# A list scheduler's model of its engines: a port shared by VectorE and GpSimd, and estimates of other lengths

## The chip, the cores and the metric

One core of one Trainium2 chip runs the whole kernel as one launch. Its engines are TensorE (PE in the profile, with PEld for the weight loads beside it), VectorE (DVE), ScalarE (ACT), GpSimd (POOL) and SyncE (SP, which here issues DMAs). Each engine works through its own instructions strictly in the order in which the program holds them, and waits on semaphores for the others. The metric is the device time of one execution in microseconds (us), less is better.

## The reference

Two transformer blocks over one sequence of 256 positions and 1024 channels, in fp32.

```
h    = rms_norm(x) @ w_in            # first block: two convolution mixers (kernels of 3 and 31), gated
x   += w_mix_out(sigmoid(gate_sc) * y_sc + sigmoid(gate_cf) * y_cf)
x   += w_xo(cross_attention(q = rms_norm(x) @ w_q, k, v = rms_norm(mem) @ w_kv))
# PEER layer: 128 x 128 = 16384 experts, 8 heads, the best 16 of each head
s    = (rms_norm(x) @ w_pq) . subkeys ; top 16 of each half, then top 16 of the 256 sums
g    = softmax(best scores)
x   += sum over the chosen experts of gelu(h . u[e]) * g * v[e]
# second block: sliding-window attention with ALiBi and sinks, latent attention with rotary angles
x   += rmsnorm((sigmoid(g_a) * out_a @ w_o_a + sigmoid(g_b) * out_b @ w_o_b) @ w_out)
x   += rmsnorm(square(relu(rmsnorm(x) @ w_up)) @ w_down)
```

The kernel does not gather experts. It computes all 16384 products `h . u[e]` (128 units U of 128 experts each), multiplies them by a gate matrix that is zero for experts that were not chosen, and multiplies by all of v (128 units V).

## The kernel before, in words

**Units.** Weights come in units of 128x1024 fp32 (`w`, one DMA of 512 KB on SP's queue). fp32 products are made out of halves: ACT copies a unit to a rounded `wh` (L288), and GpSimd or VectorE subtracts it from `w` to get the rest, `wl` (L292). PE then does 24 matmuls of 128x256 for a unit: 16 with `wh` against the high and low half of the activations, 8 with `wl`. Three buffers each of `w`, `wh` and `wl` let the splits run up to three units ahead.

**Stages,** in the order in which PE meets them: the projections of the first block with the convolutions on VectorE (L607), the cross attention, the PEER queries, the top-16 search on VectorE, 128 U units (matmuls with `hA`, `hB`; ACT makes the gelu into `Ah`, L1234), 128 V units (matmuls with `zz`, which ACT and VectorE split from `Ah`, L241 and L238), then the second block: attention, its gates `se0`, the output products, and the MLP's 64 units.

**select(t)** (L1161 to L1203), for t = 0 and 1 (128 positions each): VectorE and an Exp on ACT turn the chosen 16 of each head into softmax gates, then four times compare (L1179), multiply (L1182) and reduce (L1185) 1024 columns; PE transposes the results (L1192), ACT and VectorE copy them to `selT`. Inside `choose()` select(1) follows select(0).

**Gates** (`gbatch`, L1251 to L1268): for 8 positions VectorE builds one-hot `ohJ` (L1251), `ohI` (L1253) and two products gI (L1256); PE does 16 matmuls of 128x64 (L1264); VectorE multiplies the result into `Ah` (L1268). There are 32 such batches for each half of the experts: half 0 is spawned behind U unit 63 and needs both selects, and V unit 0 needs half 0; half 1 is spawned behind U unit 127, and V unit 64 needs half 1. Two lanes of batches alternate.

**positions()** (L1319 to L1392): rotary angles and distances for the second block, on VectorE with two Sin on ACT, spawned at V unit 72. `x1_tile(n)`, the first step of the second block, comes behind a `need` for them and for the last `zz`.

**Who goes first.** The order of each engine's instructions is not written by hand. A list scheduler (`Sched`) in Python builds it when the program is made. Each chain of steps is a generator of `Op`s; an Op has an engine (or several to choose from) and an estimated cost. The scheduler keeps a virtual time for each engine, `vt`; the step with the lowest estimated start plus priority is emitted next. Splits have priority -200, gates 300, `choose()` 600, `positions()` 1500, convolutions 1500 and more (larger is later). The loop over units calls `sch.pe(...)`, which first emits everything whose estimated start lies before PE's virtual time, and then the unit's matmuls. `need` emits until an event exists. So the costs decide what stands ahead of what on every engine, and nothing on the chip reorders it.

Of the kernel before, what the change touches and what calls it, by code (L numbers as in the profile page):

```python
# [19 lines left out]
F32 = mybir.dt.float32  # L20
# [50 lines left out]
class Sched:  # L71
# [16 lines left out]
    def est(self, co):  # L88
        op = co.op
        t = co.ready if op.chain else co.last  # L90
        for d in op.deps:
            e = self.ev.get(d)
            if e is None:
                return None
            if e > t:
                t = e
        if op.eng == "pe":
            t += self.SLACK
        if isinstance(op.eng, str):
            return max(t, self.vt[op.eng]), op.eng, op.cost  # L100
        best = None
        for eng, cost, bias in op.eng:
            st = max(t, self.vt[eng])
            if best is None or st + cost + bias < best[0]:
                best = (st + cost + bias, st, eng, cost)
        return best[1:]

    def emit(self, co, st, eng, cost):
        op = co.op
        if isinstance(op.eng, str):  # L110
            op.fn()
        else:
            op.fn(eng)
        self.vt[eng] = st + cost
        fin = st + cost + self.LAT
        if op.chain:
            co.last = co.ready
        co.ready = max(co.ready, fin)
        if op.ev is not None:
            self.ev[op.ev] = fin  # L120
        co.op = next(co.gen, None)
        if co.op is None:
            self.cos.remove(co)

    def pick(self, horizon):
        best = None
        for co in self.cos:
            e = self.est(co)
# [61 lines left out]

def c_pool(n):
    return 150 + 2.1 * n


def c_mm(n, count=1):
    return count * (max(n, 64) / 2.4 + 2.5)
# [4 lines left out]
def tile_kernel(ctx, tc, A, out):  # L201
# [33 lines left out]


# [234 lines left out]
    def hl(H, L, src, n, hev, lev):  # L471

        yield Op("act", c_act(n), act(H, src, AF.Copy), ev=hev)
        yield Op("dve", c_dve(n), lambda: V.tensor_tensor(L, src, H.bitcast(F32), op=OP.subtract), ev=lev)  # L474

    def hl_gain(H, L, src, g, n, hev, lev, deps=()):
        yield Op("act", c_act(n, 1), act(H, src, AF.Copy, scale=g), deps=deps, ev=hev)
        yield Op("dve", c_dve(n, 1),
# [107 lines left out]
    def mulR(p, R, dst, rdep, ev=None):  # L586
        return Op("dve", c_dve(S), tt(dst, p[:, :S], R, OP.mult), deps=[rdep], ev=ev)
# [37 lines left out]
    def post_g(j):  # L625
        def g(p):
# [7 lines left out]
            yield Op("dve", c_dve(S, 1),  # L634
# [16 lines left out]
    def post_x(j):  # L651
        def g(p):
# [4 lines left out]
            yield Op("dve", c_dve(S), tt(b[:, 2:2 + S], p[:, :S], scc[j], OP.mult), deps=[("scc", j)])  # L657
# [115 lines left out]
    def post_k(n):  # L773
        def g(p):
            yield Op("act", c_act(S), act(kHL[:, 0, n], p[:, :S], AF.Copy))
            yield Op("dve", c_dve(S), tt(kHL[:, 1, n], p[:, :S], kHL[:, 0, n].bitcast(F32), OP.subtract),
# [35 lines left out]
    def post_v(n):  # L812
        def g(p):
# [4 lines left out]
            yield Op("dve", c_dve(512), tt(L, src, H.bitcast(F32), OP.subtract), ev=("v", n))  # L818
# [60 lines left out]
    for key, j in order:  # L879
# [6 lines left out]
        else:  # L886
            go(u)
# [16 lines left out]
    def post_sc(n):  # L904
        def g(p):
            d = gates["gs"][:, n]
            yield Op("dve", c_dve(S), tt(d, p[:, :S], d, OP.mult), deps=[("gs", n)], ev=("m1", n))
# [64 lines left out]
    def head_xa(h):  # L972
# [15 lines left out]
        yield Op("dve", c_dve(512), lambda: V.tensor_reduce(mx[:, 0:2], b["s"].rearrange("p (t m) -> p t m", t=2),  # L988
# [21 lines left out]
        yield Op("dve", c_dve(512), lambda: V.tensor_tensor(  # L1010
# [16 lines left out]
        yield Op("dve", c_dve(512), lambda: V.tensor_tensor(  # L1027
# [110 lines left out]
    def top16(val, idx, src, tmp, n, ev=None, deps=()):  # L1138
        yield Op("dve", c_dve(n), lambda: V.max(val[:, 0:8], src), deps=deps)
        yield Op("dve", c_dve(n), lambda: V.max_index(idx[:, 0:8], val[:, 0:8], src), chain=False)  # L1140
        yield Op("dve", c_dve(n), lambda: V.match_replace(tmp, val[:, 0:8], src, LOW), chain=False)
        yield Op("dve", c_dve(n), lambda: V.max(val[:, 8:16], tmp))  # L1142
        yield Op("dve", c_dve(n), lambda: V.max_index(idx[:, 8:16], val[:, 8:16], tmp), ev=ev)  # L1143
# [12 lines left out]
    def select(t):  # L1156
# [8 lines left out]
        yield Op("dve", c_dve(128), lambda: V.tensor_reduce(sm, g3, op=OP.add, axis=AX.X))  # L1165
# [9 lines left out]
        for q, (pos, dst) in enumerate(((AFi, IF), (BFi, JF))):  # L1175
            for c in range(2):
# [8 lines left out]
                yield Op("dve", c_dve(1024), lambda eq=eq, dst=dst, c=c: V.tensor_reduce(  # L1185
# [15 lines left out]
        yield Op("dve", c_dve(128), lambda: V.scalar_tensor_tensor(  # L1201
# [41 lines left out]
    def gbatch(hh, t0, pool):  # L1243
# [209 lines left out]
    def x1_tile(n):  # L1453
        yield Op("dve", c_dve(S), tt(x1[:, n], xr[:, n], vacc[n // 2][:, (n % 2) * S:(n % 2 + 1) * S], OP.add),
# [17 lines left out]
    def x1_stats():  # L1472
# [15 lines left out]
        for n in range(8):  # L1488
            yield Op("dve", c_dve(S, 1), lambda n=n: V.scalar_tensor_tensor(
# [78 lines left out]
    def post_kr(p):  # L1568
# [13 lines left out]
        for q in range(4):  # L1582
# [3 lines left out]
            yield Op("dve", c_dve(S), lambda r=r, q=q: V.tensor_tensor(  # L1586
# [9 lines left out]
    def post_ka(p):  # L1596
        t = p[:, :S]
        yield mulR(p, RR, t, "RR")
        for q in range(2):
# [3 lines left out]
            yield Op("dve", c_dve(S), lambda r=r, q=q: V.tensor_tensor(  # L1603
                kaM[r, 1, q], t[r], kaM[r, 0, q].bitcast(F32), op=OP.subtract), ev="ka" if q == 1 else None)

    def post_va(p):
# [12 lines left out]
        yield Op("dve", c_dve(S), lambda: V.tensor_tensor(  # L1619
# [23 lines left out]
    def tail(lane, pev, free, scale):  # L1643
# [4 lines left out]
        for i in range(2):  # L1648
            yield Op("dve", c_dve(256 - 128 * i), lambda i=i: V.tensor_reduce(
# [19 lines left out]
        yield Op("dve", c_dve(384), lambda: V.tensor_tensor(  # L1669
            pT[:, 1], b[:, 0:384], pT[:, 0].bitcast(F32), op=OP.subtract), ev=("pt",) + pev)  # L1670

    def head_a(h, lane, pev, free):
# [15 lines left out]
        yield Op("dve", c_dve(384), lambda: V.scalar_tensor_tensor(  # L1688
# [29 lines left out]
    def outs(pairs, group):  # L1718
        b = LB[2 * group]
        for kind, i in pairs:  # L1720
# [15 lines left out]
            for q in range(2):  # L1736
# [3 lines left out]
                yield Op("dve", c_dve(S), lambda r=r, q=q: V.tensor_tensor(  # L1740
# [42 lines left out]
    def post_gab(j, key):  # L1783
        def g(p):
            dst = sg[key]
            yield Op("dve", c_dve(S), lambda: V.tensor_tensor(dst[:, j], p[:, :S], RR, op=OP.mult), ev=(key, "raw", j))
# [25 lines left out]
    def post_kn(n, p):  # L1812
        for q in range(2):
# [3 lines left out]
            yield Op("dve", c_dve(S), lambda r=r, q=q: V.tensor_tensor(  # L1817
# [3 lines left out]
    def post_vb(s, p):  # L1821
        yield Op("act", c_act(512), lambda: ACT.activation(vbP[:, 0, s], p, AF.Copy))
        yield Op("dve", c_dve(512), lambda: V.tensor_tensor(vbP[:, 1, s], p, vbP[:, 0, s].bitcast(F32),
# [170 lines left out]
    def fin():  # L1994
# [4 lines left out]
        for n, c in ((0, 2), (2, 2), (4, 2), (6, 2)):  # L1999
            y, xx = yg[:, n:n + c], xn[:, n:n + c]  # L2000
            yield Op("dve", c_dve(c * S, 1), tt(y, y, r.to_broadcast([128, c, S]), OP.mult),
# [109 lines left out]
```

## Time and profile before

| | us |
|---|---|
| median of 3 runs (lowest, highest) | 1803.94 (1802.5, 1808.71) |
| the profiled execution | 1811.32 |
| its span in the trace | 1809.5, granted clock 0.954 |
| PE busy | 1688.5 (93% of the span) |
| DVE, ACT, POOL busy | 1222.8 (68%), 803.3 (44%), 1185.9 (66%) |

Busy times are sums over the span, so a high share says which engine mostly sets the pace, not what each stage waits for. The granted clock is TensorE's, 1.00 for full speed. The U units lie at about 468 to 952 us, the V units at 952 to 1404 us.

### The profile page before, as it was taken

The numbers are of one execution on the slowest core, as the hardware profiler recorded it, in microseconds if no ns is written. First come the engines' busy times: TensorE is split into PE (matmuls) and PEld (weight loads), VectorE is DVE, ScalarE is ACT, GpSimd is POOL, SyncE is SP. The second block draws the span as 40 slices with busy tenths as digits, with TensorE's granted clock in tenths as the row PEclk, the third lists the DMA queues.
The fourth block names the chain that finished last, engine by engine and source line by source line (L and its number), as shares of the span: only waits on it lengthen the run. The fifth ranks groups of instructions, "written<-read, shape, count | busy, mean of one in ns | idle before, by whom it ended". The sixth has DMA issues, their size and how long they took to land.

```text
span 1809.5 us, 33154 instructions
## 1 busy us (share of the span) xinstructions
PE 1688.5 (93%) x13460; PEld 1666.1 (92%) x13460; DVE 1222.8 (68%) x1994; ACT 803.3 (44%) x1302; POOL 1185.9 (66%) x509
## 2 busy tenths in 40 slices
PE   8898989898996999999999999999999889979997
PEld 7898989898996999999999999999999878979997
DVE  7999966658998706776006777889787897474302
ACT  5533445555443442222443223444444545656533
POOL 5677865456685884444884556887688633768885
PEclk8999999999998998888999999999999999999999
DMA  6454644445453453222553334555455331545553
GB/s 200 151 175 146 192 163 141 129 129 165 148 182 115 150 179 115 94 94 94 171 180 117 115 117 129 186 180 161 152 186 181 120 102 65 165 139 176 185 187 117
DMA packets 75305, 266.73 MB, mean 147 GB/s; under 512 B 8720, under 2 KB 9232, under 8 KB 75152
## 3 DMA queue, kind: packets, MB, share of 16 engines
q1 hardware_dynamic: 73856, 262.77, 44.8%
q8 instruction: 105, 1.72, 0.4%
q10 hardware_dynamic: 1296, 1.85, 0.3%
q14 instruction: 48, 0.39, 0.1%
HBM read 262.48 MB, written 2.10 MB: 146 GB/s over the span
## 4 chain that ended last, share of the span: by engine, by line
PE 61%; DVE 33%; ACT 3%; issue 2%; DMA 1%; POOL 0%; SPq 0%; DVEq 0%; ACTq 0%; POOLq 0%
PE mmb L370 29%; PE msb L1343 7%; PE msb L1341 7%; PE msb L1345 7%; DVE msb L607 5%; PE msb L1264 4%; PE mmb L1264 4%; DVE zz L238 3%; DVE scr L1182 1%; DVE scy L662 1%; DVE scr L1143 1%; DVE scr L1140 1%; ACT wh L288 1%; DVE scr L1179 1%; DVE scr L1142 1%
## 5 line engine op out<-in xcount | busy, mean ns | idle before, releaser
L292 POOL TENSOR_TENSOR wl<-w,wh 128x1024 fp32r<-128x1024 f32 x473 | 1162.2, 2461 | 591.4 <-ACT wh L288 413.3
L288 ACT ACTIVATE wh<-w 128x1024 fp32r<-128x1024 f32 x491 | 518.4, 1059 | 587.9 <-PE msb L1343 260.1
L238 DVE TENSOR_TENSOR zz<-Ah,zz 128x256 fp32r<-128x256 f32 x128 | 216.4, 1693 | 140.0 <-ACT zz L241 140.0
L370 PE MATMUL mmb<-hA,wh 128*128 128x256 f32 x1024 | 263.8, 293 | 1.2 <-ACT wh L288 1.2
L370 PE MATMUL mmb<-hB,wh 128*128 128x256 f32 x1024 | 262.1, 291 | 0.0
L1343 PE MATMUL msb<-zz,wh 128*128 128x256 f32 x1008 | 252.1, 287 | 7.8 <-DVE zz L238 7.7
L1341 PE MATMUL msb<-zz,wh 128*128 128x256 f32 x1008 | 253.2, 288 | 0.8 <-ACT zz L241 0.8
L370 PEld LDWEIGHTS mmb<-hA,wh 128*128 128x128 f32 x1024 | 206.6, 202 | 1.4 <-ACT wh L288 1.4
L370 PEld LDWEIGHTS mmb<-hB,wh 128*128 128x128 f32 x1024 | 205.6, 201 | 0.0
L1343 PEld LDWEIGHTS msb<-zz,wh 128*128 128x128 f32 x1008 | 197.1, 196 | 8.8 <-DVE zz L238 8.8
L1341 PEld LDWEIGHTS msb<-zz,wh 128*128 128x128 f32 x1008 | 197.2, 196 | 1.0 <-ACT zz L241 1.0
L370 PE MATMUL mmb<-hA,wl 128*128 128x256 f32 x1024 | 156.3, 299 | 0.4 <-POOL wl L292 0.4
L1345 PE MATMUL msb<-zz,wl 128*128 128x256 f32 x1008 | 145.0, 287 | 0.0
L370 PEld LDWEIGHTS mmb<-hA,wl 128*128 128x128 f32 x1024 | 142.1, 205 | 0.6 <-POOL wl L292 0.6
L370 PE MATMUL mmb<-hN,wh 128*128 128x256 f32 x896 | 120.4, 286 | 13.3 <-ACT hN L241 5.5
L1345 PEld LDWEIGHTS msb<-zz,wl 128*128 128x128 f32 x1008 | 132.3, 195 | 0.0
L1264 PEld LDWEIGHTS <-ohF 128*128 128x128 f16 x1024 | 121.5, 146 | 11.2 <-DVE ohF L1256 6.0
L370 PEld LDWEIGHTS mmb<-hN,wh 128*128 128x128 f32 x896 | 113.2, 195 | 15.3 <-ACT wh L288 6.7
L607 DVE SCALAR_TENSOR_TENSOR msb<-glu,vec,msb 128x256 f32<-128x256 f32 x232 | 113.1, 487 | 6.2
L1268 DVE SCALAR_TENSOR_TENSOR Ah<-msb,Ah 128x512 f32<-128x512 f32 x32 | 22.1, 692 | 101.3 <-PE msb L1264 101.3
L1234 ACT ACTIVATE Ah<-mmb 128x256 f32<-128x256 f32 x128 | 47.1, 368 | 84.0 <-PE mmb L370 84.0
L370 PE MATMUL mmb<-eu,wh 128*128 128x256 f32 x512 | 70.7, 287 | 6.4 <-DVE uHL L474 2.7
(465 smaller groups left out, 3268.1 us busy)
## 6 DMA issues: line engine op xcount, KB each, us to landing
w<-in_peer_u_dram SPq DMA_DIRECT2D x128, 512.0 KB, 3.5
w<-in_peer_v_dram SPq DMA_DIRECT2D x128, 512.0 KB, 3.5
w<-in_w_in_dram SPq DMA_DIRECT2D x81, 512.0 KB, 3.5
w<-in_w_up_dram SPq DMA_DIRECT2D x32, 512.0 KB, 3.5
w<-in_w_down_dram SPq DMA_DIRECT2D x32, 512.0 KB, 3.5
w<-in_w_peer_q_dram SPq DMA_DIRECT2D x16, 512.0 KB, 3.7
w<-in_w_v_dram SPq DMA_DIRECT2D x8, 512.0 KB, 3.5
w<-in_sc_w_out_dram SPq DMA_DIRECT2D x8, 512.0 KB, 3.6
```

Source lines behind the costliest of these rows:

```text
L238: return lambda e="dve": ENG[e].tensor_tensor(o, a, b, op=op)
L288: yield Op("act", c_act(1024), lambda: ACT.activation(h, w, AF.Copy), deps=u["wdep"], ev=("H", u["i"]))
L292: lambda e: ENG[e].tensor_tensor(l, w, h.bitcast(F32), op=OP.subtract), ev=("L", u["i"]))
L370: PE.matmul(p[:, :S], a, b, start=first and n == 0, stop=last and n == len(todo) - 1)
L607: lambda k=k: V.scalar_tensor_tensor(cc[:, j] if k == 30 else o(), glu[:, j, k:k + S], vcol("cf_w", j * 31 + k), o(), op0=OP.mult, op1=OP. ...
L662: lambda k=k: V.scalar_tensor_tensor(y, b[:, k:k + S], vcol("sc_w", j * 3 + k), y, op0=OP.mult, op1=OP.add),
L1234: yield Op("act", c_act(S), lambda: ACT.activation(Ah[n // 64][:, n % 64], p[:, :S], AF.Gelu), ev=("U", n))
L1264: PE.matmul(b[0][:, t * 64:(t + 1) * 64], ohJ[:, :, t], gI[i][:, :, t], start=i == 0, stop=i == 1)
L1268: yield Op("dve", c_dve(512), lambda: V.scalar_tensor_tensor(z, b[0].rearrange("p (t i) -> p i t", t=8), 1.0 / GS, z, op0=OP.mult, op1=OP. ...
L1341: PE.matmul(o, u["H"][:, d, :], opH, start=first and d % 2 == 0, stop=False, skip_group_check=True)
L1343: PE.matmul(o, u["H"][:, d, :], opL, start=False, stop=False, skip_group_check=True)
L1345: PE.matmul(o, u["L"][:, d, :], opH, start=False, stop=last, skip_group_check=True)
```

## The change: what it does

A step on VectorE or GpSimd that reads SBUF gets a cost of class `Shared`; the scheduler keeps one more time, `port`, and estimates such a step to begin neither before its engine nor before the port is free. Steps with an operand in PSUM (`c_psum`) and single-input searches and reductions (`c_one`) are exempt. Nearly all estimates get other lengths. Some 30 Ops change only which cost function they call; the gates' matmuls go from an estimated 16 x 30 ns to 16 x 140 ns. One `need(["R0"])` is put before the second unit of the gates' projection in the first block, and a list `busy` keeps a generator from being emitted twice. No instruction computes anything else: PE's instructions keep their count, VectorE has 1837 in place of 1852 and GpSimd 528 in place of 514, since the scheduler also chooses the engine of some steps. All 18 `wl` of 128x1024 that VectorE made are GpSimd's after the change.

```diff
+        self.port = 0.0
+        self.busy = []
...
         if isinstance(op.eng, str):
-            return max(t, self.vt[op.eng]), op.eng, op.cost
+            return self.begins(t, op.eng, op.cost), op.eng, op.cost
         best = None
         for eng, cost, bias in op.eng:
-            st = max(t, self.vt[eng])
+            st = self.begins(t, eng, cost)
...
+    def begins(self, t, eng, cost):
+
+        t = max(t, self.vt[eng])
+        return max(t, self.port) if isinstance(cost, Shared) else t
...
         self.vt[eng] = st + cost
+        if isinstance(cost, Shared):
+            self.port = max(self.port, st + cost)
...
+class Shared(float):
+    pass
+
+
 def c_dve(n, ap=0, fast=False):
-    return 66 + n / (1.92 if fast else 0.96) + 60 * ap
+    return Shared(66 + 60 * ap + n / 0.96 if not fast else 96 + 60 * ap + n / 1.75)
+
+
+def c_one(n, ap=0):
+    return 66 + n / 0.96 + 60 * ap
 
 
 def c_psum(n, ap=0):
-    return 130 + n / 0.96 + 40 * ap
+    return 155 + n / 0.96 + 60 * ap
 
 
 def c_act(n, ap=0):
-    return 93 + n / 1.2 + 93 * ap
+    return 145 + n / 1.12 + 93 * ap
 
 
 def c_pool(n):
-    return 150 + 2.1 * n
+    return Shared(150 + 2.2 * n)
 
 
 def c_mm(n, count=1):
-    return count * (max(n, 64) / 2.4 + 2.5)
+    return count * max(n / 2.4 + 13, 110)
...
-        yield Op((("pool", 2303.0, u.get("bias", -2000.0)), ("dve", c_dve(1024), 0.0)),
+        yield Op((("pool", c_pool(1024), u.get("bias", -2000.0)), ("dve", c_dve(1024), 0.0)),
                  lambda e: ENG[e].tensor_tensor(l, w, h.bitcast(F32), op=OP.subtract), ev=("L", u["i"]))
...
+            if (key, j) == ("g", 1):
+                sch.need(["R0"])
             go(u)
...
-        yield Op("pe", 16 * 30.0, f, ev=("Gp", hh, t0))
+        yield Op("pe", 16 * 140.0, f, ev=("Gp", hh, t0))
         z = Ah[hh][:, :, sl]
-        yield Op("dve", c_dve(512), lambda: V.scalar_tensor_tensor(
+        yield Op("dve", c_psum(512), lambda: V.scalar_tensor_tensor(
```

**The selects, on ACT.** Here stands ACT's order before, at U unit 43: the last gelus ahead of select(0)'s transposes (`selT`), and the Exp of select(1) (`scr<-scr`).

```order
L1234 ACTIVATE Ah_5368<-mmb 128x256
L1196 ACTIVATE selT<-msb 128x128
L1197 ACTIVATE selT<-msb 128x128
L1200 ACTIVATE selT<-msb 128x128
L241 ACT_TABLE_LOAD
L241 ACTIVATE scr<-scr 128x128
L288 ACTIVATE wh<-w 128x1024
L1234 ACT_TABLE_LOAD
```

After the change the same stands once on ACT, with line numbers some 25 higher; the two gelus of the first row are those of U units 62 and 63.

```order
L1261 ACTIVATE Ah_5337<-mmb 128x256 x2
L265 ACT_TABLE_LOAD
L265 ACTIVATE scr<-scr 128x128
L1223 ACTIVATE selT<-msb 128x128
L1224 ACTIVATE selT<-msb 128x128
L1227 ACTIVATE selT<-msb 128x128
L265 ACTIVATE scr<-scr 128x128
L1223 ACTIVATE selT<-msb 128x128
L1224 ACTIVATE selT<-msb 128x128
L1227 ACTIVATE selT<-msb 128x128
L312 ACTIVATE wh<-w 128x1024 x2
```

So the Exp of select(0), which stood among the gelus some twelve units ahead of its transposes, now stands behind the gelu of unit 63, and select(1) runs right behind. On PE the U matmuls before were cut 792, 232 and 2048 (with the three transposes of a select at each cut); after the change all six transposes stand together behind 1536 U matmuls, which are units 0 to 63.

**The gates, on VectorE.** These are the first batches of half 0 before the change, two of them in each turn, behind select(1)'s last row.

```order
L1203 CAST selT<-scr 128x128
L1251 TENSOR_TENSOR ohF<-selT 128x1024 x2
L1253 TENSOR_TENSOR ohF<-selT 128x512
L1256 TENSOR_TENSOR ohF<-ohF,selT 128x512 x2
L1253 TENSOR_TENSOR ohF<-selT 128x512
L1256 TENSOR_TENSOR selT<-ohF,selT 128x512 x2
L1268 SCALAR_TENSOR_TENSOR Ah_5368<-msb,Ah_5368 128x64x8 x2
```

After the change a turn of two batches reads so on VectorE.

```order
L1278 TENSOR_TENSOR ohF<-selT 128x1024
L1280 TENSOR_TENSOR ohF<-selT 128x512
L1283 TENSOR_TENSOR ohF<-ohF,selT 128x512
L1295 SCALAR_TENSOR_TENSOR Ah_5337<-msb,Ah_5337 128x64x8
L1283 TENSOR_TENSOR ohF<-ohF,selT 128x512
L1278 TENSOR_TENSOR ohF<-selT 128x1024
L1280 TENSOR_TENSOR ohF<-selT 128x512
L1283 TENSOR_TENSOR selT<-ohF,selT 128x512 x2
L1295 SCALAR_TENSOR_TENSOR Ah_5337<-msb,Ah_5337 128x64x8
```

The multiply into `Ah` (L1295) of an earlier batch now stands between the two gI of a later one. On PE, half 0 before was 16 groups of 32 gate matmuls with 48 U matmuls between them; now it is one block of 512 gate matmuls behind all U matmuls. Half 1 before was cut into 16s between V matmuls (40 and 8 in turn); now 16 gate matmuls stand behind the first 40 V matmuls, and the other 496 in one block behind V unit 63.

**The angles, on VectorE.** Before the change they stood among the splits `zz` of V units; this is their end, with the first steps of the second block.

```order
L1326 TENSOR_SCALAR RpD<-angS 128x256
L238 TENSOR_TENSOR RpD<-RpD,angS 128x384
L1329 TENSOR_SCALAR angS<-RpD 128x384
L238 TENSOR_TENSOR RpD<-RpD,angS 128x384
L238 TENSOR_TENSOR zz<-Ah_7687,zz 128x256 x44
L238 TENSOR_TENSOR x_15244<-xr,msb 128x256 x2
```

Now the last 64 `zz` come first, then all of `positions()`; this is its beginning.

```order
L262 TENSOR_TENSOR zz<-Ah_7688,zz 128x256 x64
L1399 CAST angS<-angS 128x256
L1400 TENSOR_SCALAR angS<-angS,cst 128x256
L1403 TENSOR_SCALAR angS<-angS 128x256
L1405 TENSOR_SCALAR angS<-angS 128x256
```

And its end now stands right ahead of the second block.

```order
L1353 TENSOR_SCALAR RpD<-angS 128x256
L262 TENSOR_TENSOR RpD<-RpD,angS 128x384
L1356 TENSOR_SCALAR angS<-RpD 128x384
L262 TENSOR_TENSOR RpD<-RpD,angS 128x384
L262 TENSOR_TENSOR x_15244<-xr,msb 128x256 x6
```

So 44 `zz` lay between the angles and `x1_tile(0)`, and none does now. In the first stage and in the second block's attention the order changes in many small places: the memory's normalisation and the convolutions' place on VectorE, and on PE the gate units of `se0`, which now stand earlier among the attention heads.

## Rows read from the trace of the kernel before

**Rows 1.** The page's head: busy time by engine (share of the span), instructions.

```profile
PE 1688.5 (93%) x13460; PEld 1666.1 (92%) x13460; DVE 1222.8 (68%) x1994; ACT 803.3 (44%) x1302; POOL 1185.9 (66%) x509
```

**Rows 2.** Windows by stage: length, busy time of each engine (instructions), granted clock, DMA.

```profile
468.00:685.00 217.00, 197.69 (x1588) 196.45 (x1588) 143.66 (x379) 96.38 (x146) 166.65 (x65) 0.94 0.48 156
685.00:952.00 267.00, 261.39 (x2007) 259.43 (x2005) 129.33 (x152) 84.58 (x126) 154.72 (x63) 0.90 0.38 125
952.00:1404.00 452.00, 441.26 (x3589) 438.60 (x3590) 360.82 (x339) 183.04 (x270) 311.92 (x128) 0.98 0.47 152
1113.00:1226.00 113.00, 113.00 (x944) 113.00 (x943) 93.55 (x41) 53.28 (x78) 92.32 (x40) 1.00 0.56 178
0.00:300.00 300.00, 268.50 (x2097) 261.42 (x2098) 258.14 (x459) 141.53 (x217) 200.29 (x101) 0.95 0.51 166
1404.00:1554.00 150.00, 130.07 (x1024) 125.88 (x1023) 118.15 (x251) 83.31 (x191) 72.12 (x33) 0.97 0.32 103
```

**Rows 3.** Timeline of DVE in select(1): start, length, instruction, [idle before].

```profile
583.40 0.28 DVE L1161 TENSOR_TENSOR scr<-scr 128x128 f32<-128x128 f32 x1
584.55 0.29 DVE L1165 TENSOR_REDUCE scr<-scr 128x8 f32<-128x128 f32 x1 [0.87 <-ACT scr L241]
...
585.52 0.22 DVE L1171 TENSOR_SCALAR scr<-scr 128x128 uint32<-128x128 uint32 x1
...
591.49 0.22 DVE L1172 CAST scr<-scr 128x128 f32<-128x128 uint32 x1
...
592.02 1.22 DVE L1179 TENSOR_TENSOR scr<-scr,cst 128x1024 f32<-128x1024 f32 x1
...
595.67 2.17 DVE L1179 TENSOR_TENSOR scr<-scr,cst 128x1024 f32<-128x1024 f32 x1
```

**Rows 4.** Timeline of PE behind select(0)'s transposes.

```profile
581.56 0.69 PE L1192 MATMUL msb<-cst,scr 128*128 128x128 f32 x2 [9.67 <-DVE scr L1185]
581.90 0.56 PE L370 MATMUL mmb<-hA,wh 128*128 128x256 f32 x1
...
587.10 0.28 PE L370 MATMUL mmb<-hA,wh 128*128 128x256 f32 x1
```

**Rows 5.** Timeline of ACT at select(1)'s Exp.

```profile
582.92 1.28 ACT L241 ACT_TABLE_LOAD   x1
```

**Rows 6.** Timeline of PE at the last two gate batches of half 0.

```profile
853.12 2.14 PE L1264 MATMUL msb<-ohF 128*128 128x64 f16 x16
...
856.95 2.05 PE L370 MATMUL mmb<-hA,wl 128*128 128x256 f32 x8
```

**Rows 7.** Timeline of DVE within gates of half 0.

```profile
738.34 0.42 DVE L1253 TENSOR_TENSOR ohF<-selT 128x512 f16<-128x512 f16 x1
738.79 0.76 DVE L1256 TENSOR_TENSOR selT<-ohF,selT 128x512 f16<-128x512 f16 x2
...
744.78 0.69 DVE L1268 SCALAR_TENSOR_TENSOR Ah<-msb,Ah 128x512 f32<-128x512 f32 x1 [1.25 <-PE msb L1264]
745.39 1.28 DVE L1251 TENSOR_TENSOR ohF<-selT 128x1024 f16<-128x1024 f16 x2
746.59 0.42 DVE L1253 TENSOR_TENSOR ohF<-selT 128x512 f16<-128x512 f16 x1
```

**Rows 8.** Timeline of DVE: angles, the last split, the first x1 tile.

```profile
1234.13 0.29 DVE L1376 TENSOR_SCALAR angS<-angS 128x256 f32<-128x256 f32 x1
1234.46 2.51 DVE L1378 TENSOR_SCALAR angS<-angS 128x256 f32<-128x256 f32 x1
...
1392.57 2.43 DVE L238 TENSOR_TENSOR zz<-Ah,zz 128x256 fp32r<-128x256 f32 x1 [0.45 <-ACT zz L241]
1399.28 0.75 DVE L238 TENSOR_TENSOR x<-xr,msb 128x256 f32<-128x256 f32 x2 [4.29 <-PE msb L1406]
```

**Rows 9.** Groups of instructions: the splits `wl` by engine.

```profile
L292 POOL TENSOR_TENSOR wl<-w,wh 128x1024 fp32r<-128x1024 f32 x473 | 1162.2, 2461 | 591.4 <-ACT wh L288 413.3
L292 DVE TENSOR_TENSOR wl<-w,wh 128x1024 fp32r<-128x1024 f32 x18 | 36.4, 2022 | 18.4 <-ACT wh L288 18.4
```

More of the change, by code (lines that the diff above doesn't have):

```diff
@@ L106, in est @@
         return best[1:]
+    def begins(self, t, eng, cost):
+        t = max(t, self.vt[eng])
+        return max(t, self.port) if isinstance(cost, Shared) else t
     def emit(self, co, st, eng, cost):
         op = co.op
+        self.busy.append(co)
         if isinstance(op.eng, str):
@@ L113, in emit @@
             op.fn(eng)
+        self.busy.remove(co)
         self.vt[eng] = st + cost
+        if isinstance(cost, Shared):
+            self.port = max(self.port, st + cost)
         fin = st + cost + self.LAT
@@ L127, in pick @@
         for co in self.cos:
+            if co in self.busy:
+                continue
             e = self.est(co)
@@ L234, in once, with banked @@
         return f
+    def banked(ap):
+        return ap.space == PSUM
     def tt(o, a, b, op):
@@ L473, in hl @@
         yield Op("act", c_act(n), act(H, src, AF.Copy), ev=hev)
-        yield Op("dve", c_dve(n), lambda: V.tensor_tensor(L, src, H.bitcast(F32), op=OP.subtract), ev=lev)
+        yield Op("dve", c_psum(n) if banked(src) else c_dve(n),
+                 lambda: V.tensor_tensor(L, src, H.bitcast(F32), op=OP.subtract), ev=lev)
     def hl_gain(H, L, src, g, n, hev, lev, deps=()):
         yield Op("act", c_act(n, 1), act(H, src, AF.Copy, scale=g), deps=deps, ev=hev)
-        yield Op("dve", c_dve(n, 1),
+        yield Op("dve", c_psum(n, 1) if banked(src) else c_dve(n, 1),
                  lambda: V.scalar_tensor_tensor(L, src, g, H.bitcast(F32), op0=OP.mult, op1=OP.subtract), ev=lev)
@@ L586, in mulR @@
     def mulR(p, R, dst, rdep, ev=None):
-        return Op("dve", c_dve(S), tt(dst, p[:, :S], R, OP.mult), deps=[rdep], ev=ev)
+        return Op("dve", c_psum(S), tt(dst, p[:, :S], R, OP.mult), deps=[rdep], ev=ev)
     glu = P1.tile([128, 8, 30 + S], F32, name="glu")
@@ L817, in g @@
             yield Op("act", c_act(512), act(H, src, AF.Copy))
-            yield Op("dve", c_dve(512), tt(L, src, H.bitcast(F32), OP.subtract), ev=("v", n))
+            yield Op("dve", c_psum(512), tt(L, src, H.bitcast(F32), OP.subtract), ev=("v", n))
         return g
@@ L906, in g @@
             d = gates["gs"][:, n]
-            yield Op("dve", c_dve(S), tt(d, p[:, :S], d, OP.mult), deps=[("gs", n)], ev=("m1", n))
+            yield Op("dve", c_psum(S), tt(d, p[:, :S], d, OP.mult), deps=[("gs", n)], ev=("m1", n))
         return g
@@ L1138, in top16 @@
     def top16(val, idx, src, tmp, n, ev=None, deps=()):
[L1139 to L1143, printed above, removed]
+        yield Op("dve", c_one(n), lambda: V.max(val[:, 0:8], src), deps=deps)
+        yield Op("dve", c_one(n), lambda: V.max_index(idx[:, 0:8], val[:, 0:8], src), chain=False)
+        yield Op("dve", c_one(n), lambda: V.match_replace(tmp, val[:, 0:8], src, LOW), chain=False)
+        yield Op("dve", c_one(n), lambda: V.max(val[:, 8:16], tmp))
+        yield Op("dve", c_one(n), lambda: V.max_index(idx[:, 8:16], val[:, 8:16], tmp), ev=ev)
     def topk_head(h):
@@ L1164, in select @@
         sm = SM[:, t * 16:t * 16 + 8]
-        yield Op("dve", c_dve(128), lambda: V.tensor_reduce(sm, g3, op=OP.add, axis=AX.X))
+        yield Op("dve", c_one(128), lambda: V.tensor_reduce(sm, g3, op=OP.add, axis=AX.X))
         yield Op("dve", 130.0, lambda: V.reciprocal(sm, sm))
@@ L1453, in x1_tile @@
     def x1_tile(n):
-        yield Op("dve", c_dve(S), tt(x1[:, n], xr[:, n], vacc[n // 2][:, (n % 2) * S:(n % 2 + 1) * S], OP.add),
+        yield Op("dve", c_psum(S), tt(x1[:, n], xr[:, n], vacc[n // 2][:, (n % 2) * S:(n % 2 + 1) * S], OP.add),
                  ev=("x1", n))
@@ L1648, in tail @@
         for i in range(2):
-            yield Op("dve", c_dve(256 - 128 * i), lambda i=i: V.tensor_reduce(
+            yield Op("dve", c_one(256 - 128 * i), lambda i=i: V.tensor_reduce(
                 mx[:, i:i + 1], src[:, sl[i][0]:sl[i][1]], op=OP.max, axis=AX.X))
@@ L1687, in head_a @@
                  chain=False)
-        yield Op("dve", c_dve(384), lambda: V.scalar_tensor_tensor(
+        yield Op("dve", c_psum(384), lambda: V.scalar_tensor_tensor(
             pr[:, 1:385], b[:, 0:384], 0.125, pr[:, 1:385], op0=OP.mult, op1=OP.add))
@@ L1785, in g @@
             dst = sg[key]
-            yield Op("dve", c_dve(S), lambda: V.tensor_tensor(dst[:, j], p[:, :S], RR, op=OP.mult), ev=(key, "raw", j))
+            yield Op("dve", c_psum(S), lambda: V.tensor_tensor(dst[:, j], p[:, :S], RR, op=OP.mult), ev=(key, "raw", j))
         return g
```

34 lines of the change are left out of this document (17 added, 17 removed).

## The prediction, on record before the run

> **What bounds the kernel now.** I read the page's head first: PE is busy for 1688.5 us, 93%, and no other engine over 68% [rows 1]. PE sets the pace, so a change of order is worth what PE idles, or runs slowly, more or less. Then I read windows by stage, for PE's count and clock. Where nothing disturbs it, 944 matmuls of 128x256 take 113.00 us at clock 1.00 [rows 2], 0.1197 us each. That is the yardstick: what a stage takes beyond its matmuls at this pitch is its loss. Last came the timelines at the three places at which the order of before and after differ most: what each instruction takes alone, and what it takes beside a GpSimd split.
>
> The U stage up to the gates takes 217 us [rows 2], for 1576 matmuls (792, 232 and 552 by the order), 188.6 us: a loss of 28, of which 0.3 lies before the first U matmul and 0.7 are transposes; I take 27.4. From there to the V stage are 267 us [rows 2] for 1496 matmuls (179.1) and half 0 of the gates. Two gate batches take from 853.12 to 856.95 us [rows 6], so a batch 1.92 and a half 61.3: a loss of 26.6. V has 452 us [rows 2] for 3072 matmuls and 5 that follow (368.3) and another 61.3: a loss of 22.4. The first 300 us hold 2097 matmuls, mostly of this size, 251 us: a loss of 49, with DVE busy for 258.14 of the 300 [rows 2]. In the second block's attention PE is busy for 130.07 of 150 us [rows 2].
>
> **What the change does: the selects.** Before, a select ran on DVE under U matmuls, and PE met its transposes only near its end. Now the Exp of select(0) stands behind the gelu of unit 63 on ACT, and PE's next instructions are the transposes of both selects. Nothing is left on PE to hide them, and no U unit ahead on ACT. The cost of one select alone: 583.40 to the end of L1171 at 585.74 is 2.34 us, the casts from 591.49 to 592.02 are 0.53, and one compare, multiply and reduce is 592.02 to 595.67, 3.65 us, of which there are four [rows 3]: 17.5 us. GpSimd is then idle as well, its three buffers full, so I take these undisturbed lengths. For select(0) the part ahead of L1165 (1.15 us [rows 3]) is done early; in its place come gelu, table load (1.28 us [rows 5]) and Exp, some 2 us. From the transposes to select(1)'s first step are 581.56 to 583.40 [rows 3, 4], 1.84. Sum: 2 + 16.35 + 1.84 + 17 + 0.35 for the last transposes = 37.5 us of idle PE. Then PE starts at the slow clock: the unit behind select(0) took from 581.90 to 587.10 [rows 4], 5.2 instead of 2.9 us, 2.3 more. Together 39.8 against 27.4 lost before: **+12.4**.
>
> **The gates.** Before, U or V matmuls lay between batches while DVE prepared the next ones. Now half 0 is one block of 512 gate matmuls, half 1 nearly so, and DVE sets their pace. A batch costs DVE 0.60 (ohJ, 745.39 to 746.59 for two), 0.45 (ohI), 0.76 (two gI) and 0.61 (STT, 744.78 to 745.39) [rows 7], together 2.42 us against PE's 1.92. It isn't all overlapped: by the order of a pair, STT of the batch before stands ahead of the second gI, so once in two batches PE waits for STT (0.61), one gI (0.38) and hand-overs between the engines, for which I choose 0.8. A pair then takes 3.83 + 1.79 = 5.62 us, and 32 batches 90 us, a loss of 28.7. The lower bound is DVE's own sum, 77 us (loss 16); the upper is no overlap of DVE and PE, 139 us (loss 78). I stay near the lower, because the order does let the next one-hots be made while PE works.
>
> Half 0 loses 28.7 in place of 26.6: **+2.1**. The reason that it is so little is that before PE ran the 48 U matmuls between two groups at the slow clock (eight `wl` matmuls took 2.05 us behind the gates [rows 6], where the pitch gives 0.96; clock 0.90 in the stage [rows 2]). In V, before, the gates cost almost nothing beyond their own time. Now V loses 28.7 and twice a slow start of 2.3 (behind each block): 33.3 in place of 22.4, **+10.9**, with the angles' share of the old loss gone.
>
> **The angles.** They follow the last `zz`, and `x1_tile(0)` follows them by force of the `need`; PE has nothing else. Their DVE steps are some 40, at about 0.29 us each when alone and up to 2.51 beside a split [rows 8]; summed in their short lengths they are 12.5 us, and two Sin with a table load (1.28 [rows 5]) add some 2. The last `zz` ended at 1395.0 [rows 8]; GpSimd still makes `wl` until PE stops, and I choose two of these delays, 4 us. So `x1_tile(0)` begins at about 1413 instead of 1399.28 [rows 8], and PE begins as much later: **+14**. Bounds: +9 (no delay, some steps earlier) and +24 (six delays).
>
> **The 18 wl.** DVE gives up 36.4 us (2022 ns each), and GpSimd takes 2461 ns for each [rows 9]. Where DVE sets the pace this frees it, but other DVE steps then meet GpSimd's split and wait it out, as the angle step of 2.51 us did [rows 8]. I take 0, with -20 (ten of them lie in the first 300 us and the attention) and +22 as bounds (below).
>
> **The first stage and the attention.** R0's statistics, the memory's normalisation and the convolutions only change places; the first stage loses 49 us and both signs are open, so I take 0, between -15 and +12. In the attention, gate units that covered the later heads now stand earlier; I take +4 between -10 and +20 (the 20 us of idle double). The new `need` moves PE's statistics behind 72 rather than 40 matmuls, which is inside this.
>
> **Sum:** 12.4 + 2.1 + 10.9 + 14 + 4 = 43.4. The profiled execution took 1811.3 us and its median runs 1803.9, 7.4 less; on the trace's scale the sum is 1854.7, on that of the median 1847.
>
> **Rivals.** (a) *Faster:* the freed DVE and the truer estimates shorten the first stage. For: 49 us are lost there, 20 in the attention, and DVE is the busy engine. Against: the order moves little work out of DVE there. It decides once these two give back more than 43 + 5 us out of their 69; at 55 the time is 1792. 8%.
>
> (b) *The blocks run at DVE's sum,* 2.42 us a batch: each block gains 12.6, and the time is 1822. For: the one-hots have two buffers. Against: the STT between the two gI. 12%.
>
> (c) *The blocks run slower,* because splits for the next units meet DVE's steps. Rows 7 hold the undisturbed lengths only; a long step of 2.5 us at every fourth batch makes each block some 16 us longer: 1879. Against: PE consumes no U or V unit in a block, so GpSimd stops after three. 10%.
>
> (d) *The port.* On the chip a split on GpSimd keeps it for 2.46 us, on DVE 1.22 where it is alone, as any of 1024 columns there (592.02 [rows 3]; the mean is 2.02 [rows 9]). If every moved split delays a needed DVE step by the difference of 1.24, 18 of them cost 22 us: 1869. For: the pair 0.29 and 2.51 us of one kind of step [rows 8]. Against: GpSimd is idle for a third of the span [rows 1], and PE isn't waiting for DVE in all stages. 10%. The Trainium skill's page "SBUF — State Buffer", section "Who interferes with whom", states this as a lock: a VectorE instruction that reads two SBUF inputs, or uses both ports for one, and a GpSimd instruction exclude each other for the whole instruction. The trace agrees with it for the angle step; by that rule alone, each split moved to the slower engine would lengthen the port's work, and the sum would be that of (d).
>
> (e) *No change in the time:* the model of the port adds no wait on the chip, and the pieces cancel. It needs -43 from the open terms. 4%.
>
> **Chances.** The forecast 56%, its own range 1833 to 1862. Within 0.3% (5.4 us), about what a measurement of this kernel can tell from no change, lies (e) alone; faster are (a) and a tail of the open terms, 10%; slower 86%. Below 1812 lie (a), (e) and little else, and above 1878 the upper half of (c) and the tail of (d), so the range goes from 1812 to 1878.
>
> **What would show it.** PE idle near 652 to 690 us, for some 37 us, waiting for L1212's reduce; two blocks with only gate matmuls of about 90 us, with the clock near half speed; `x1_tile(0)` some 14 us behind where the V stage ends. If the blocks last 77 us, (b) is right; if DVE's steps in them show lengths of 2.5 us, (c). If the span up to the U stage is over 20 us shorter, (a). It would be wrong if PE found other work in these places, or if the first 468 us moved by more than the terms allow.

## The result, and the profile after

The changed kernel takes 1862.97 us (median of 4 runs, 1861.17 to 1865.70), the kernel before, run beside it, 1806.33: a ratio of 1.031 (95% interval 1.028 to 1.035), slower by 57 us. The profiled execution of after has a span of 1863.9 us against 1809.5.

Where the 54 us between the two spans lie is read from the first and last start of a tile's matmuls (`hA` for U, `zz` for V, `se0a` and `me0a` for the second block). V ends when its last matmul makes room for the next one:

| stretch | before | after | difference | forecast |
|---|---|---|---|---|
| to the first U matmul | 468.3 | 466.0 | -2.3 | 0 |
| U and half 0 of the gates | 484.2 | 491.5 | +7.3 | +14.5 |
| V and half 1 | 450.9 | 455.8 | +4.9 | +10.9 |
| end of V to the first se0 matmul | 0 | 14.5 | +14.5 | +14 |
| attention, first se0 to first me0 matmul | 173.2 | 205.0 | +31.8 | +4 |
| the rest | 232.9 | 231.1 | -1.8 | 0 |

The page's slices come first: PE's busy tenths and its clock, a slice being 46.6 us.

```profile
PE   7989999889999929999889999899996688889997
PEclk9989999999999959999569998579998898889999
```

Two pairs of slices stand at a clock of 5 to 7 tenths with PE at 8 or 9 (the blocks of gates), one at 2 tenths busy (the selects), and one stretch at 6 to 8 (the attention). The waits of PE name them: total in us, how often, and the longest.

```profile
PE msb L1219 <- DVE scr L1212: 36.0, 4, 11.4
PE mmb L394 <- ACT se0a L265: 14.3, 1, 14.3
PE msb L1291 <- DVE ohF L1283: 13.9, 30, 1.3
PE mmb L1291 <- DVE selT L1283: 12.8, 30, 0.7
```

The windows, cut at the borders of the stages, have the columns of [rows 2].

```profile
652.00:695.00 43.00, 8.52 (x45) 7.59 (x46) 38.29 (x50) 5.53 (x13) 3.79 (x2) 0.56 0.05 17
695.00:875.00 180.00, 180.00 (x1502) 179.96 (x1501) 7.24 (x4) 82.74 (x126) 150.25 (x63) 1.00 0.56 183
875.00:957.50 82.50, 67.44 (x512) 61.58 (x510) 72.69 (x153) 1.73 (x4) 2.39 (x1) 0.53 0.04 14
1146.00:1226.00 80.00, 66.02 (x500) 60.10 (x498) 69.22 (x147) 1.01 (x3) 2.59 (x2) 0.53 0.04 14
1413.00:1428.00 15.00, 0.65 (x5) 0.45 (x3) 13.99 (x28) 2.94 (x7) 6.97 (x5) 0.62 0.11 36
1428.00:1633.00 205.00, 169.58 (x1220) 162.69 (x1221) 131.87 (x287) 100.21 (x213) 90.71 (x39) 0.86 0.29 94
```

The reader is to see four things. In the selects DVE works for 38 of 43 us while PE waits. Between them and the first block U runs at full pace, 1502 matmuls in 180 us. In the blocks, of 82.5 and 80 us, DVE is busy for 72.69 and 69.22 us, and the clock is near half. In the attention PE needs 205 us for the 1220 matmuls that took 173.2 before; it is busy for 169.6 us at clock 0.86 and idle for 35.

The same window of the kernel before, from the first se0 to the first me0 matmul, reads so.

```profile
1403.40:1576.60 173.20, 153.27 (x1220) 149.08 (x1219) 131.17 (x281) 96.48 (x209) 90.53 (x41) 0.97 0.35 112
```

Half of the 31.8 us is idle time (35.4 instead of 19.9). The other half is that PE is busy for longer with the same matmuls (169.6 instead of 153.3), at a lower clock (0.86 instead of 0.97). The lowest clocks stand where PE idles most: here is the worst of the 20 us windows, with 10 us of work at clock 0.57.

```profile
1448.00:1468.00 20.00, 9.95 (x47) 9.37 (x46) 9.25 (x18) 7.19 (x14) 5.79 (x4) 0.57 0.24 80
```

### The profile page after: what moved, and what is told of

It reads as the page before. It is cut to its first block, busy times and chain, and to the rows that moved or that the text cites. A ratio compares the mean times of both kernels' runs of the same rounds, so it can differ in the third digit from the quotient of the medians.

```text
span 1863.9 us, 33160 instructions
## 1 busy us (share of the span) xinstructions
PE 1685.6 (90%) x13460; PEld 1653.4 (89%) x13460; DVE 1125.1 (60%) x1979; ACT 804.0 (43%) x1302; POOL 1199.0 (64%) x523
## 5 line engine op out<-in xcount | busy, mean ns | idle before, releaser
L316 POOL TENSOR_TENSOR wl<-w,wh 128x1024 fp32r<-128x1024 f32 x491 | 1183.0, 2413 | 642.9 <-ACT wh L312 427.8
L262 DVE TENSOR_TENSOR zz<-Ah,zz 128x256 fp32r<-128x256 f32 x128 | 288.6, 2259 | 59.9 <-ACT zz L265 59.8
L394 PE MATMUL mmb<-hA,wh 128*128 128x256 f32 x1024 | 252.9, 285 | 0.0
L394 PE MATMUL mmb<-hB,wh 128*128 128x256 f32 x1024 | 252.6, 284 | 0.0
L394 PEld LDWEIGHTS mmb<-hB,wh 128*128 128x128 f32 x1024 | 197.9, 193 | 0.0
L394 PEld LDWEIGHTS mmb<-hA,wh 128*128 128x128 f32 x1024 | 197.8, 193 | 0.0
L394 PE MATMUL mmb<-hA,wl 128*128 128x256 f32 x1024 | 144.2, 284 | 0.0
L394 PEld LDWEIGHTS mmb<-hA,wl 128*128 128x128 f32 x1024 | 132.6, 193 | 0.0
L1295 DVE SCALAR_TENSOR_TENSOR Ah<-msb,Ah 128x512 f32<-128x512 f32 x32 | 22.0, 687 | 181.0 <-PE msb L1291 181.0
L265 ACT ACTIVATE zz<-Ah 128x256 fp32r<-128x256 f32 x128 | 50.9, 402 | 162.5 <-DVE Ah L1295 159.8
```

What stands on the lines that cost most here:

```text
L262: return lambda e="dve": ENG[e].tensor_tensor(o, a, b, op=op)
L265: return lambda e="act": ACT.activation(o, a, f, **kw)
L394: PE.matmul(p[:, :S], a, b, start=first and n == 0, stop=last and n == len(todo) - 1)
L1295: yield Op("dve", c_psum(512), lambda: V.scalar_tensor_tensor(z, b[0].rearrange("p (t i) -> p i t", t=8), 1.0 / GS, z, op0=OP.mult, op1=OP ...
```

## The experiments

All ratios are to the kernel before, run beside the experiment on the same chip. The changed kernel was not run again beside them, so differences from it are between sets of runs; in these sets the median of the kernel before lay between 1804.3 and 1808.5 us. A stage with the same order differed by up to 3 us between two profiled executions (U with half 0 of the gates took 491.5 us in the changed kernel and 494.4 in experiment 5), and the attention, with the same order of PE, by 1.4 (after, 4, 6 and 9).

**1. The new lengths without the port.**

```diff
-        return max(t, self.port) if isinstance(cost, Shared) else t
+        return t
```

> The changed kernel with its new lengths, but the scheduler's port taken away again (a step begins when its engine is free). Theory (the port in the model starves VectorE's low-priority work, so selects, gates and angles go out late): they are back among U and V matmuls, and the time is 1795 to 1815 us. Rival (the new lengths do it): 1850 us or more. What the attention does is open in both; if its loss comes from the new lengths, 20 to 30 us of the 57 stay, 1826 to 1836.

Measured: 1809.1 us, ratio 1.0024 (1.0007 to 1.0040). Selects, gates and angles are back among the matmuls, and all but 5 us of the loss is gone. In the trace U with half 0 is 467.8 us (16 less than before), the attention 178.9 (5.7 more than before).

**2. The port with the old lengths.**

```diff
-    return Shared(66 + 60 * ap + n / 0.96 if not fast else 96 + 60 * ap + n / 1.75)
+    return Shared(66 + n / (1.92 if fast else 0.96) + 60 * ap)
...
-        yield Op("pe", 16 * 140.0, f, ev=("Gp", hh, t0))
+        yield Op("pe", 16 * 30.0, f, ev=("Gp", hh, t0))
```

(and `c_psum`, `c_act`, `c_pool` and `c_mm` as before the change)

> The other half: the port kept, all lengths back to those of before (VectorE, PSUM, ScalarE, GpSimd, matmuls, gates). Theory: the same blocks as in the changed kernel, 1850 to 1875 us. Rival (the new lengths do it): 1800 to 1815 us.

Measured: 1900.9 us, ratio 1.055 (1.052 to 1.058), beyond what either side had expected. Up to the end of V the order of PE has the same cuts as in the changed kernel, and yet the run is 38 us slower than that. The waits of PE in this run say where.

```profile
PE msb L1291 <- DVE ohF L1283: 31.1, 15, 2.4
PE mmb L1291 <- DVE selT L1283: 30.3, 15, 2.1
```

A block lasts some 99 us instead of 81: two batches go out at once and DVE prepares the next two only behind them, so in each block PE waits 15 times for 2 us. The estimate of 480 ns for a batch is the likely reason, but it was not put back alone here. The attention takes 203.9 us, nearly the 205.0 of the changed kernel, so its loss comes with the port and without the new lengths too. The two experiments together show that the port makes the loss, and that with the port the new lengths take 38 us of it back, 36 of them in the two blocks of gates.

**3. The angles asked for early.**

```diff
         if n == 110:
+            sch.need(["csk", "dist"])
             sch.spawn(warm(), prio=1500.0)
```

> The changed kernel with a need for the angles and distances at V unit 110, so that they go out among V units; the order of the second block is the same row for row. Theory A (the 14.6 us gap ahead of the second block is simply moved under PE's matmuls): 1848 to 1851 us. Theory B (in the V stage a GpSimd split of 2.41 us and a zz of 0.42 us already fill the port for 2.83 of the 2.87 us of a unit, so 12.5 us of VectorE steps lengthen V by nearly as much): 1858 to 1863 us. In both the attention keeps its 32 us, unless late angles are its cause too: then 1820 us.

Measured: 1859.2 us, ratio 1.032 (1.029 to 1.036), no different from the changed kernel's. The gap of 14.5 us is gone, and V is 471.9 instead of 455.8 us. One window of V shows the price.

```profile
1360.00:1380.00 20.00, 6.48 (x44) 6.08 (x44) 17.47 (x37) 6.37 (x11) 7.06 (x3) 0.72 0.28 94
```

PE is busy for 6.5 of 20 us, since `need` puts all angle steps ahead of the next `zz`. The time is that of theory B, but its reason, a port that is full beside V, is not shown by this: the placing alone makes PE wait. The attention took 199.6 us here, so late angles are some 5 of its 32.

**4. The selects asked for early.**

```diff
+        if n == 40:
+            sch.need([("sel", 0)])
+        if n == 52:
+            sch.need([("sel", 1)])
         if n == 64:
```

> The changed kernel with select(0) asked for at U unit 40 and select(1) at unit 52. Theory (two selects in a row with PE idle cost some 39 us, and under U matmuls part of them is hidden, as the 27 us lost before): 9 to 13 us less, 1850 to 1854 us. Rival (beside GpSimd splits a select takes so long that nothing is won): 1860 to 1866 us.

Measured: 1863.4 us, ratio 1.034 (1.031 to 1.037): nothing won. The wait is unchanged.

```profile
PE msb L1219 <- DVE scr L1212: 36.2, 4, 11.4
```

The time is the rival's, but not for the reason that I had given. A `need` emits the whole chain at one place, the Exp behind the gelu of the last unit on ACT and the transposes ahead of the next unit on PE, so PE waits as long at unit 40 as at unit 64. The splits stop as well, so a select ran here without them. Beside splits, in experiment 9, the same step does run slowly, as these rows of experiments 4 and 9 show.

```profile
581.26 1.22 DVE L1206 TENSOR_TENSOR scr<-scr,cst 128x1024 f32<-128x1024 f32 x1
576.73 3.42 DVE L1207 TENSOR_TENSOR scr<-scr,cst 128x1024 f32<-128x1024 f32 x1
```

My edit moved the stall and hid nothing; experiment 9 is the better one.

**5. No port in the second block.**

```diff
+    sch.share = False
     p3 = ExitStack()
```

(`begins` looks at the port only while `sch.share` is true; so in 9 and 11)

> The changed kernel up to the end of the V stage row for row; from the second block on the scheduler no longer looks at the port (the new lengths stay). Theory (the 32 us lost in the attention come from the port's order there): the stretch from the first se0 to the first me0 matmul falls from 205 us to 176 to 183, the time to 1833 to 1842 us. Rival (they come from the late angles or the new lengths): it keeps over 195 us, the time 1853 us or more.

Measured: 1843.3 us, ratio 1.019 (1.016 to 1.022), 20 us less than the changed kernel and 1 us above the expected range. The attention fell from 205.0 to 182.3 us; its window:

```profile
1428.00:1611.00 183.00, 161.17 (x1224) 155.64 (x1225) 136.25 (x292) 100.27 (x213) 87.08 (x37) 0.93 0.33 107
```

So the port's order makes 23 of the 32 us. By the orders, before 264 se0 matmuls stood behind the first score of a second-kind head (`kne1a`), after the change 56, here 200; and after the change 5 of 8 such blocks of scores stood behind the first output product, here none. That the lack of this cover is what costs the time fits with the count in all thirteen traces: with 264 behind that score the attention took 170 to 173 us (before, 7, 8, 10, 11), with 200 179 and 182 (1 and 5), with 56 200 to 206 (after, 3, 4, 6, 9) and with none 204 (2). It was not tried alone, and from 56 to none nothing more is lost.

PE's order from the attention on is the same in experiments 1 and 5, instruction for instruction; the angles come late only in 5. So the 9 us that stay in 5 split into 3.4 with the late angles (182.3 against 178.9) and 5.7 with the new lengths (178.9 against 173.2).

**6. The gates ahead of the splits.**

```diff
-        sch.spawn(a, prio=300.0)
-        sch.spawn(b, prio=300.0)
+        sch.spawn(a, prio=-600.0)
+        sch.spawn(b, prio=-600.0)
```

> The changed kernel with the gates' priority at -600 in place of 300, ahead of the splits at -200; selects and angles stay late. The order then has the gates of both halves in groups of 16 to 64 among U and V matmuls. Theory (each block of gates alone loses 19 to 21 us plus a slow start of some 3): half 1 is hidden as before, about 20 us less; half 0 gains where groups are short and PE keeps its clock: 1830 to 1846 us. Rival (VectorE and the port are full beside V units, so gates among them lengthen V as much as a block does): 1855 to 1866 us.

Measured: 1849.9 us, ratio 1.023 (1.020 to 1.026), 13 us less than the changed kernel, between the ranges of theory and rival, and not where the theory had it. V takes 458.3 us, no less than with a block; U with half 0 takes 481.2, 10 less. Three windows show why, two of half 0 and one of half 1.

```profile
695.00:745.00 50.00, 50.00 (x368) 49.70 (x367) 33.88 (x53) 12.32 (x17) 20.46 (x9) 0.86 0.30 95
745.00:795.00 50.00, 50.00 (x415) 49.52 (x413) 47.82 (x55) 14.39 (x20) 28.16 (x10) 1.00 0.29 96
951.00:1080.00 129.00, 119.50 (x858) 116.56 (x858) 95.34 (x171) 19.50 (x29) 35.87 (x15) 0.76 0.21 66
```

In the second window the order has 16 gate matmuls and 24 U matmuls in turn, and the clock stays at 1.00. In the first, and in half 1, groups of 32 and up to 64 gate matmuls stand in a row, and the mean clock is 0.86 and 0.76.

**7. The kernel before with one estimate changed.**

```diff
-        yield Op("pe", 16 * 30.0, f, ev=("Gp", hh, t0))
+        yield Op("pe", 16 * 140.0, f, ev=("Gp", hh, t0))
```

> The kernel before with one number changed, the estimate of a gate batch on PE from 16 x 30 to 16 x 140 ns. On PE the groups of 32 gate matmuls in half 0 become groups of 16 with 8 and 16 U matmuls between, where the first run without the port lost almost nothing. Theory (that number alone brings what the new lengths gained in the U stage, 16 us): 1784 to 1793 us. Rival (it was the other lengths, or it is lost elsewhere): 1800 to 1808 us.

Measured: 1787.8 us, ratio 0.989 (0.986 to 0.991), 20 us faster than the kernel before. U with half 0 is 461.5 us instead of 484.2, V 4.8 us longer. Half 0 now has groups of 16, with 8 and 16 U matmuls between them in turn, and its clock is near 1 all through:

```profile
685.00:735.00 50.00, 50.00 (x400) 49.36 (x398) 48.12 (x72) 10.57 (x15) 19.12 (x8) 0.97 0.24 81
735.00:785.00 50.00, 50.00 (x411) 49.36 (x410) 49.52 (x71) 10.21 (x14) 20.34 (x8) 1.00 0.23 74
```

**8. The same, with the angles in the U stage.**

```diff
+        if n == 50:
+            angS[0] = epool.tile([128, 8, S], F32, tag="e0a", name="angS")
...
+            sch.spawn(positions(), prio=700.0, ready=sch.vt["pe"] + 3000.0)
...
+            sch.need(["csk", "dist"])
             ohF[0] = epool.tile([128, 4096], HF, tag="e0a", name="ohF")
```

(and the spawn at V unit 72 is gone)

> The run before this one, with the angles and distances moved into the U stage (spawned at U unit 50, needed at unit 64), where VectorE idles behind the selects and no zz shares the port. Theory (in V they cost 13 us because the port is full there): 10 to 14 us less than the run before, 1772 to 1782 us. Rival (they were hidden in V, or now hold up the gates): no less, 1785 to 1793 us.

Measured: 1782.2 us, ratio 0.985 (0.981 to 0.988), the fastest of all together with run 11. V fell by 13.7 us to 442.0, as the theory had it, but U with half 0 grew by 7.2 to 468.7, where PE now waits 4.7 us for the first one-hots. Both sides have part of it; against run 7 the intervals overlap.

**9. No port from the PEER queries to the gates.**

```diff
+    sch.share = False
     sch.spawn(choose(), prio=600.0)
...
+            sch.share = True
             ohF[0] = epool.tile([128, 4096], HF, tag="e0a", name="ohF")
```

> The changed kernel with the port looked at everywhere but from the first U unit to U unit 64: both selects stand among U matmuls again (688, 192 and 2192), and gates, angles and attention stay as the change put them. Theory (the selects' term: 41 us lost in the first half of U, against 33 in the first run without the port): 6 to 14 us less than the changed kernel, 1849 to 1857 us. Rival (a select beside splits is so slow that its place doesn't matter): 1860 to 1866 us.

Measured: 1858.0 us, ratio 1.027 (1.025 to 1.030). The edit lets the port go some 70 us before the first U unit, with the queries, and not only there as I had expected. PE's wait for the selects is 19.0 us instead of 36.0, and from the first U matmul to the first gate 402.1 us instead of 408.8. The theory holds in the trace, at its lower end; the time lies between its range and the rival's, at the edge of what can be told.

**10. All `wl` on GpSimd.**

```diff
-        yield Op((("pool", 2303.0, u.get("bias", -2000.0)), ("dve", c_dve(1024), 0.0)),
+        yield Op((("pool", 2303.0, u.get("bias", -1e9)),),
```

> The kernel before with every wl of 128x1024 on GpSimd, as after the change; the scheduler is otherwise that of before, and the rest of the order moves only a little. Theory (the term taken as 0): within 6 us of before, 1798 to 1810 us. Rival (d) of the prediction (each split moved takes the port 1.24 us longer and delays VectorE): 1815 to 1830 us. Rival on the other side (VectorE freed of 36 us in stages that wait for it): 1785 to 1797 us.

Measured: 1801.8 us, ratio 0.997 (0.996 to 0.999): 5 us faster, within the first theory's range. Rival (d) falls, as far as the order of the kernel before can show it.

**11. The port only up to the mix projection, on run 8.**

```diff
+    sch.share = False
     go_pair(u_mix[0], u_mix[1], lambda k: ("mg", k))
```

> The eighth run (gate estimate, angles in the U stage) with the port kept in the scheduler up to the mix projection and let go there, with the lengths of before. In the changed kernel the last matmul of the convolution stage ended 12 us earlier than before, and what followed it took longer. Theory (the port's order helps where VectorE's shared steps are the bound and no low-priority step is waited for): 8 to 14 us less than the eighth run, 1766 to 1775 us. Rival (the gain there is lost again before the U stage, as in the changed kernel, or was another execution's luck): 1778 to 1785 us.

Measured: 1782.6 us, ratio 0.987 (0.985 to 0.989), the same as run 8. The rival holds: the convolution stage ended at 294.1 us, 3.7 earlier than in run 8 and not 12, and the U stage began 3.2 earlier.

## Why the prediction was right, and where a size was off

The sign was right, and so was the mechanism at three places: selects, gates and angles went out late and PE waited for them. But by the table they make 27 of the 54 us, where 39 were forecast, and the attention makes 31.8, where 4 were. That the forecast of 1847 us is only 16 short of 1863 is in part luck: the gates were priced some 13 us too dear, which hides half of what the attention was priced too cheap. The time also lies 1 us above the forecast's own range of 1833 to 1862, in a part of the whole range that was there for (c) and (d), and neither came. Point by point:

**The selects** were sized well. The predicted stall of 37.5 us was 36.0, on the line named. From 466.0 to 874.8 us U lost 41 us beyond its 3072 matmuls at the pitch of [rows 2], against 39.8 forecast.

**The gates** were sized too dear. I chose 0.8 us for hand-overs in a pair of batches; the timeline of DVE in the first block shows less. It answers to [rows 7].

```profile
919.98 0.42 DVE L1280 TENSOR_TENSOR ohF<-selT 128x512 f16<-128x512 f16 x1
...
920.77 0.68 DVE L1295 SCALAR_TENSOR_TENSOR Ah<-msb,Ah 128x512 f32<-128x512 f32 x1
...
923.87 0.69 DVE L1295 SCALAR_TENSOR_TENSOR Ah<-msb,Ah 128x512 f32<-128x512 f32 x1 [0.34 <-PE msb L1291]
...
925.07 0.42 DVE L1280 TENSOR_TENSOR ohF<-selT 128x512 f16<-128x512 f16 x1
```

A pair takes 919.98 to 925.07, 5.1 us instead of 5.62: DVE waits once, 0.34 us, and is else hardly idle. A block is 16 x 5.1 = 82 us, nearer to rival (b) than I had it (2.55 us a batch; (b) had 2.42, I had 2.81). By the prediction's yardstick half 0 lost 21 us (82.8 instead of 61.3) where it had lost 26.6 before: the block was cheaper than the cuts among U matmuls, not dearer. In the first block DVE's steps have their lengths of [rows 7] but for one of 1.76 us at its start, beside the last split, and in the second all have them, so rival (c) falls.

**The angles** came out at 14.5 us against 14, by other parts than I had chosen, so this hit is luck. Of these rows, the first are the last `zz` and the first steps; the cast is one of `distances()`, and the last rows are what GpSimd does beside it.

```profile
1402.44 2.43 DVE L262 TENSOR_TENSOR zz<-Ah,zz 128x256 fp32r<-128x256 f32 x1 [0.45 <-ACT zz L265]
1404.79 0.28 DVE L1399 CAST angS<-angS 128x256 f32<-128x256 int32 x1
1405.11 2.51 DVE L1400 TENSOR_SCALAR angS<-angS,cst 128x256 f32<-128x256 f32 x1
...
1416.81 4.94 DVE L1347 CAST angS<-angS 128x256 f32<-128x256 int32 x1
...
1426.71 2.07 DVE L262 TENSOR_TENSOR x<-xr,msb 128x256 f32<-128x256 f32 x6
...
1416.57 2.39 POOL L316 TENSOR_TENSOR wl<-w,wh 128x1024 fp32r<-128x1024 f32 x1 [9.11 <-ACT wh L312]
1418.91 1.80 POOL L1560 MEMSET krM<- 128x2048 f32 x1
1420.65 0.95 POOL L1560 MEMSET kaM<- 128x1024 f32 x1
1421.55 2.00 POOL L1563 MEMSET kne1a<- 128x1024 f32 x2
```

The cast, 0.29 us when alone, ends 0.15 us behind the second memset: it stood through a split and two memsets of the second block, which the prediction did not have in its sum. Together DVE's steps were held up for some 9 us instead of the 4 that I had chosen. Against this, the last `zz` ended 8.4 us ahead of the end of V instead of 4.3, so PE's last matmuls hid more of the angles.

**The attention** is the step that failed: "I take +4 between -10 and +20". It cost 31.8, outside its own bounds, and the +4 was worked out from nothing. My upper bound had PE's idle time doubling, which is about what happened (19.9 to 35.4 us); I had not priced that PE, with so much idle time, is at the slow clock in between: 16 us more for the same matmuls. Experiment 5 puts 23 us of the term on the port's order. Of the other 9, 5.7 come with the new lengths and 3.4 with the late angles, each from one pair of profiled executions.

**The first stage** came out at -2.3. Rival (a) falls: DVE was busy for 322 us instead of 378 in the first 468, and the convolution stage ended 12 us earlier, but what followed it (cross attention and queries) took 10 us longer. The same order up to there began U between 460.5 and 466.0 us in five profiled executions (after and 3 to 6), so differences of a few us in this stretch are not told apart.

**The 18 wl** at 0, and rival (d): experiment 10 measured -5 us for the move. The page "SBUF — State Buffer" of the Trainium skill, section "Who interferes with whom", tells of a lock for the whole instruction; the step of 2.51 us, which began beside a split and ended 0.16 us behind it, and the cast agree with that. The sum that I drew from it in (d), a longer time for each split that moves, did not come; presumably what the port takes longer was not waited for, which no run shows by itself.

**Why the port makes the order so late** is argued from the code and borne out by experiments 1, 2, 5 and 9. In the model a split holds the port for 2403 ns of the 2872 ns by which PE's virtual time grows in a unit. When the port comes free at a time P, a gate step could begin at once and has the key P + 300; the next split can begin only some 469 ns later, but its key is P + 469 - 200 = P + 269. The split is emitted first and moves the port behind itself, so the gap ahead of it is lost to the gates, and more so to the selects (600) and angles (1500). They come when a `need` stops PE, with nothing on PE beside them.

## What to carry to other kernels

A truer resource in a greedy list scheduler can make a worse order: where a high-priority stream nearly fills the resource, everything else is put off until something waits for it, and then it lies bare. Look in the new order for work that has moved to just ahead of its consumer, and price the stall there; and give each stall the slow clock that goes with it, not only its own length (in the attention that was half of the cost). When a wrong estimate and a missing resource are corrected together, run each alone: here one estimate, that of the gates' matmuls, was worth 20 us in the right direction.

## What the runs showed of the hardware that I had not expected

With one and the same mixture, the clock went with how gate matmuls are grouped between large ones. This window is of the kernel before, within half 0, 32 gate matmuls and 48 large ones in turn; its clock is 0.83.

```profile
700.00:750.00 50.00, 48.67 (x355) 48.22 (x355) 39.55 (x47) 12.51 (x19) 22.94 (x9) 0.83 0.25 85
```

With 16 and 24 in turn 415 matmuls fitted into the same 50 us at 1.00 (experiment 6). The 1.3 us of idle time here are not what sets the clock apart: in the first window of experiment 6, with groups of 32, PE was never idle and the clock was 0.86. Experiment 7 gained 1.1% with groups of 16, though there the mixture changed as well, with fewer large matmuls between. And a VectorE cast of 0.29 us was held for 4.94 us, by several GpSimd instructions in a row, memsets among them, and not only by one split.
